# Log decays of a gated linear attention: running sums by VectorE in place of matmuls with level matrices

## The chip, the core and the metric

One Trainium2 chip, one core. A time is the device time of one execution in microseconds (us), lower is better. Engines: PE is TensorE, DVE VectorE, ACT ScalarE, POOL GpSimd, SP SyncE, whose queue issues the DMAs. "PEld" is PE's weight load.

## What is computed

One layer of a hybrid decoder on 256 prompt tokens and 8 x 4 sample tokens (288 columns in all). The change touches the gated linear attention (GLA) only, 4 heads of key dim 256 and value dim 512:

```python
log_a = jax.nn.log_sigmoid((ag @ w_a2 + b_a).astype(f32)) / GLA_GATE_NORM     # GATE_NORM 16
...
b = jnp.cumsum(log_a, axis=2)                 # along the tokens of a chunk
b_last = b[:, :, -1:]
q_i = q * jnp.exp(b)
k_i = k * jnp.exp(-b)
k_d = k * jnp.exp(b_last - b)
A = jnp.where(causal, jnp.einsum('bnlhk,bnmhk->bnhlm', q_i, k_i), 0.0)
o_intra = jnp.einsum('bnlhm,bnmhv->bnlhv', A, v)
...
S = dc[..., None] * S + jnp.einsum('blhk,blhv->bhkv', kc, vc)
```

Both kernels compute it in an equivalent form with another chunking: products of two decays are taken at four levels (across the two blocks of 128 tokens, across halves of 64, across halves of 32, inside 32), so that every exponent is a difference of sums over a short stretch.

## The kernel before

**The frame.** `gemm` multiplies every weight of the layer with the 288 columns. A weight chunk `raw` (128x1024) is loaded by SP, each half is split into `whi` (ACT, a cast, L226) and `wlo` (DVE, raw minus whi, L172), and PE runs 12 matmuls of 288 columns on it (L248 to L250: high with high, high with low, low with high, for four output tiles). `whi` and `wlo` have 5 buffers each; a `gemm` owns 4 PSUM tiles "mm", one for each output tile, and the next `gemm` uses the same four. DVE empties each (`ya<-mm`, `sgg<-mm`) at the end of a `gemm`, so the next `gemm`'s first matmul into a tile waits for that. Its first and last chunks go tile by tile, so that the four tiles end one after another.

**GLA between the chunks.** `gla(h)` and `gla_sample(h)` are generators: `pump` runs them a step at a time between chunks, 1.25 and 0.5 steps for each chunk. So each engine's queue, which it works off strictly in order, holds weight splits and GLA work mixed. Where in the mix an instruction stands is set by the framework's scheduler at build time. The heads 0 to 3 start in the gemms gs2, ps0, gg0 and gg2.

**The decays before.** `gla` computes the gate with tokens on partitions: `pl` (two matmuls of 256 columns, L601) and `pls` (sample tokens, L602), then `log_sigmoid` (three activations and one DVE operation for each), then a split into `lah` and `lal`. Sums along the tokens are matmuls with constant 0, 1/16, -1/16 matrices: for each of the two key halves t and each block, `lah` and `lal` meet `lev` (512 columns, L634) in the bank `pc`, whose columns come out with keys on partitions. ACT takes exp of all 512 columns into `e`, exp of the negative of 128 into `en`, and for block 1 `kd` and `tot`. DVE multiplies these by q and k, and PE forms the score bank `pa` (L662 to L673). `gla_sample` does the same for the sample tokens with `levs` and the bank `pcs` (L730), whose four records for a head are two matmuls.

**Small loads.** POOL issues `norms`, `ident`, `bm` and `levs` near the start, SP `lraw` (the source of `lev`) behind the first gemm's weights. The next head's gate weights `w2r` (buffer of their own) are loaded by SP.

Of the kernel before, what the change touches and what calls it, by code (L numbers as in the profile page):

```python
# [19 lines left out]
P = 128  # L20
# [66 lines left out]
def constants():  # L87
# [28 lines left out]
    c["masks"] = ms.reshape(P, 4 * 288)  # L116
    s, o = t[:, None], t[None, :]
    a = 1.0 / 16.0
    l128a = np.where(s > o, a, 0)
    l128b = np.where(s <= o, a, 0)  # L120

    def level(w):
        blk = (s // (2 * w)) == (o // (2 * w))
        up = (o % (2 * w)) >= w
        sup = (s % (2 * w)) >= w
        return np.where(blk & up & sup & (s <= o), a, 0) + np.where(blk & ~up & ~sup & (s > o), a, 0)

    mid = 15
    same = (s // 32) == (o // 32)
    dg = np.where(same & (o % 32 > mid) & (s % 32 > mid) & (s <= o), a, 0) - np.where(  # L130
        same & (o % 32 < mid) & (s % 32 <= mid) & (s > o), a, 0)
    lv = [level(64), level(32), dg]
    c["lev"] = np.concatenate([l128a] + lv + [l128b], axis=1).astype(f)
    ts = np.arange(TS)
    s, o = ts[:, None], ts[None, :]
    sb = (s // NS) == (o // NS)
    c["levs"] = np.concatenate([np.where(sb & (s <= o), a, 0), np.where(sb & (s > o), a, 0)], axis=1).astype(f)
    rep = t % 32
    c["bm"] = np.concatenate([
# [8 lines left out]
def step_kernel(ctx: ExitStack, tc: tile.TileContext, a: dict):  # L148
# [10 lines left out]
    def bank(name):  # L159
        return psm.tile([P, 512], F32, name=name, tag="sm")  # L160
# [10 lines left out]
    def sub(out, x, y, eng=V):  # L171
        eng.tensor_tensor(out, x, y, ALU.subtract)  # L172
# [404 lines left out]

    def log_sigmoid(ps, n, w, tag, bufs=1):
        t = gpool.tile([P, w], F32, name="ls", tag=tag, bufs=bufs)
        S.activation(t[:n], ps, AF.Abs)  # L580
        S.activation(t[:n], t[:n], AF.Exp, scale=-1.0)
        S.activation(t[:n], t[:n], AF.Ln, bias=1.0)
        V.scalar_tensor_tensor(t[:n], ps, 0.0, t[:n], ALU.min, ALU.subtract)
        return t

    def gla(h):
        zq, zk = (lambda t: zqk[h][:, t]), (lambda t: zqk[h][:, 2 + t])
        yield
        w2r = gpool.tile([P, 256], F32, name="w2r")
        w2 = gpool.tile([P, 256], F32R, name="w2")  # L590
# [7 lines left out]
        yield  # L598
        pl, pls = bank("pl"), bank("pls")
# [26 lines left out]
        for t in range(2):  # L626
            e = main.tile([P, 8, P], F32, name="e", tag=f"Za{2 + t}")
            en = gpool.tile([P, 2, P], F32, name="en", tag="en", bufs=2)
            kd = gpool.tile([P, 2, P], F32, name="kd", tag="kd", bufs=2)
            tot = gpool.tile([P, 2], F32, name="tot", tag="tot", bufs=2)  # L630
            for blk in range(2):
                pc = bank("pc")
# [21 lines left out]
            mul(ev[:, :, 2], ev[:, :, 2], q2)
            mul(en, en, k2)
            mul(kd[:, 1], kd[:, 1], k2[:, 1])
            V.tensor_scalar(kd[:, 0], e[:, 0], tot[:, 1:2], None, ALU.mult)
# [57 lines left out]
    def gla_sample(h):  # L715
        zk = lambda t: zqk[h][:, 2 + t]
        while h not in ready:
            yield
        vr, las = ready[h]
        vs = gpool.tile([P, 512], F32R, name="vs")  # L720
# [12 lines left out]
        pc3 = pc[:, :128].rearrange("p (a b) -> p a b", a=2)  # L733
# [327 lines left out]
```

## Time and profile before

| what | value |
|---|---|
| median of 3 runs | 1817.43 us (1816.79 to 1817.61) |
| the profiled execution: its time, its span | 1817.1 us, 1815.3 us |
| PE busy | 1799.6 us, 99% |
| DVE busy | 1090.0 us, 60% |
| ACT busy | 862.1 us, 47% |
| POOL busy | 84.9 us, 5% |
| granted TensorE clock | nine tenths or more in every slice |

Busy time is the union of an engine's instructions. The chain of waits is followed back from the last instruction, in each step to what released it; its pieces add up to the span. Where an engine's instructions overlap (each is drawn with its fill and drain), the distance from one start to the next, called a step below, is what one costs its queue.

### The profile page before, as it was taken

The numbers are of one execution on the slowest core, as the hardware profiler recorded it, in microseconds if no ns is written. First come the engines' busy times: TensorE is split into PE (matmuls) and PEld (weight loads), VectorE is DVE, ScalarE is ACT, GpSimd is POOL, SyncE is SP. The second block draws the span as 40 slices with busy tenths as digits, with TensorE's granted clock in tenths as the row PEclk, the third lists the DMA queues.
The fourth block names the chain that finished last, engine by engine and source line by source line (L and its number), as shares of the span: only waits on it lengthen the run. The fifth ranks groups of instructions, "written<-read, shape, count | busy, mean of one in ns | idle before, by whom it ended". The sixth has DMA issues, their size and how long they took to land.

```text
span 1815.3 us, 34272 instructions
## 1 busy us (share of the span) xinstructions
PE 1799.6 (99%) x13551; PEld 1754.0 (97%) x13551; DVE 1090.0 (60%) x2004; ACT 862.1 (47%) x1618; POOL 84.9 (5%) x97
## 2 busy tenths in 40 slices
PE   8999999999999999999999999999999999999997
PEld 7999998998999989999999999999999999999997
DVE  7886575675665666766567554455545554455544
ACT  5566464443453654654444553345433553345443
POOL 2000000100100101000023000000000000000002
PEclk9999999999999999999999999999999999999999
DMA  7735447657557466544654555444454555444452
GB/s 271 244 117 165 138 156 244 205 172 246 186 186 261 146 217 242 164 166 154 225 169 162 169 161 167 169 166 163 163 171 166 163 163 173 165 163 165 161 174 87
DMA packets 92304, 324.31 MB, mean 179 GB/s; under 512 B 11056, under 2 KB 12752, under 8 KB 92144
## 3 DMA queue, kind: packets, MB, share of 16 engines
q1 hardware_dynamic: 91728, 321.26, 52.6%
q8 instruction: 106, 1.74, 0.4%
q10 hardware_dynamic: 288, 0.74, 0.1%
q14 instruction: 54, 0.44, 0.1%
q0 software_dynamic: 128, 0.14, 0.0%
HBM read 298.43 MB, written 23.66 MB: 177 GB/s over the span
## 4 chain that ended last, share of the span: by engine, by line
PE 98%; DVE 1%; DMA 0%; ACT 0%; DVEq 0%; SPq 0%; issue 0%
PE mm L248 30%; PE mm L250 30%; PE mm L249 30%; PE pu L781 1%; PE pos L772 1%; PE pst L702 1%; PE score L397 0%; PE pc L634 0%; PE po L695 0%; PE ssq L258 0%; DMA x<-in_x 0%; PE pt L426 0%; DVE wlo L172 0%; PE o L436 0%; DVE x L166 0%; PE pa L668 0%
## 5 line engine op out<-in xcount | busy, mean ns | idle before, releaser
L172 DVE TENSOR_TENSOR wlo<-raw,whi 128x512 fp32r<-128x512 f32 x1040 | 722.5, 706 | 621.0 <-ACT whi L226 618.9
L226 ACT CAST whi<-raw 128x512 fp32r<-128x512 f32 x1040 | 632.2, 619 | 852.7 <-PE mm L249 804.5
L248 PE MATMUL mm<-hh,whi 128*128 128x288 f32 x1472 | 440.1, 299 | 1.2 <-ACT whi L226 1.2
L250 PE MATMUL mm<-hh,wlo 128*128 128x288 f32 x1472 | 433.8, 295 | 2.3 <-DVE wlo L172 2.2
L249 PE MATMUL mm<-hl,whi 128*128 128x288 f32 x1472 | 433.5, 295 | 0.0
L250 PE MATMUL mm<-uh,wlo 128*128 128x288 f32 x1024 | 302.0, 295 | 0.0
L250 PE MATMUL mm<-h2h,wlo 128*128 128x288 f32 x1024 | 301.9, 295 | 0.0
L248 PE MATMUL mm<-h2h,whi 128*128 128x288 f32 x1024 | 301.9, 295 | 0.0
L248 PE MATMUL mm<-uh,whi 128*128 128x288 f32 x1024 | 301.9, 295 | 0.0
L249 PE MATMUL mm<-ul,whi 128*128 128x288 f32 x1024 | 301.7, 295 | 0.0
L249 PE MATMUL mm<-h2l,whi 128*128 128x288 f32 x1024 | 301.7, 295 | 0.0
L248 PEld LDWEIGHTS mm<-hh,whi 128*128 128x128 f32 x1472 | 276.3, 188 | 6.8 <-issue 2.2
L250 PEld LDWEIGHTS mm<-hh,wlo 128*128 128x128 f32 x1472 | 276.1, 188 | 3.5 <-DVE wlo L172 3.0
L249 PEld LDWEIGHTS mm<-hl,whi 128*128 128x128 f32 x1472 | 276.3, 188 | 2.7 <-issue 0.7
L250 PEld LDWEIGHTS mm<-uh,wlo 128*128 128x128 f32 x1024 | 192.3, 188 | 0.0
L250 PEld LDWEIGHTS mm<-h2h,wlo 128*128 128x128 f32 x1024 | 192.3, 188 | 0.0
L249 PEld LDWEIGHTS mm<-ul,whi 128*128 128x128 f32 x1024 | 192.1, 188 | 0.1
L249 PEld LDWEIGHTS mm<-h2l,whi 128*128 128x128 f32 x1024 | 192.1, 188 | 0.1
L248 PEld LDWEIGHTS mm<-h2h,whi 128*128 128x128 f32 x1024 | 192.0, 188 | 0.1
L248 PEld LDWEIGHTS mm<-uh,whi 128*128 128x128 f32 x1024 | 192.0, 188 | 0.1
L250 PE MATMUL mm<-yh,wlo 128*128 128x288 f32 x256 | 75.5, 295 | 0.0
L250 PE MATMUL mm<-gh,wlo 128*128 128x288 f32 x256 | 75.5, 295 | 0.0
(276 smaller groups left out, 1834.2 us busy)
## 6 DMA issues: line engine op xcount, KB each, us to landing
raw<-in_w SPq DMA_DIRECT2D x519, 512.0 KB, 3.3
raw<-in_s SPq DMA_DIRECT2D x32, 512.0 KB, 4.3
out_ssn<-raw SPq DMA_DIRECT2D x32, 512.0 KB, 2.8
x<-in_x SPq DMA_DIRECT2D x4, 576.0 KB, 5.9
out_sp<-so SPq DMA_DIRECT2D x8, 256.0 KB, 2.4
x<-in_x SPq DMA_DIRECT2D x7, 288.0 KB, 7.7
kc<-in_kc SPq DMA_DIRECT2D x2, 512.0 KB, 5.1
out_kcn<-kc SPq DMA_DIRECT2D x2, 512.0 KB, 5.8
```

The lines of the kernel that those rows point to most:

```text
L172: eng.tensor_tensor(out, x, y, ALU.subtract)
L226: S.copy(hi, raw)
L248: T.matmul(o, lhsT=hi[:, sl], rhs=xh(k), start=k == 0, stop=False)
L249: T.matmul(o, lhsT=hi[:, sl], rhs=xl(k), start=False, stop=False)
L250: T.matmul(o, lhsT=lo[:, sl], rhs=xh(k), start=False, stop=k == nk - 1)
L702: T.matmul(pst, lhsT=kdt[:, blk, P * t:P * t + P], rhs=vt[:, blk], start=blk == 0, stop=blk == 1)
L772: T.matmul(pos[r:r + 32], lhsT=qm[:, t, 32 * (b0 + g):32 * (b0 + g) + 32], rhs=st[g][:, 512 * t:512 * t + 512], start=b0 == 0, stop=b0 == ...
L781: T.matmul(pu, lhsT=km[:, P * t:P * t + P], rhs=vs, start=True, stop=True)
```

## The change

The gate is computed with keys on partitions at once (`w2` becomes the stationary operand, `zag` with all 288 tokens the moving one, one bank for each key half). `running` is DVE's running sum: it goes along the columns, multiplies the sum so far by `keep` (0 at the start of each run of 32 prompt tokens or 4 sample tokens, else 1) and adds the next column. The level sums are then differences of these prefix sums `pfx` and of the ends of runs, made by DVE; the factor 1/16 moves into the exponentials. `lev`, `levs`, their loads, `lah`, `lal`, `pls`, `pc` and `pcs` are gone; `seg` (128x288, 144 KB) takes the place of `levs` (32x64, 8 KB) in POOL's queue. `w2r` shares the buffer of `vtok`, so a next head's load waits until the last state matmul of the head ahead has read `vtok`; behind it in SP's queue stands that state's own store. `gla` has one more yield.

```diff
+    c["seg"] = np.tile(np.where(tok < TP, tok % 32 != 0, tok % NS != 0).astype(f), (P, 1))
...
-    G.dma_start(levs, a["levs"])
+    G.dma_start(seg, a["seg"])
...
-        SY.dma_start(lraw, a["lev"])
-        S.copy(lev, lraw)
...
+    def running(out, keep, x):
+        V.tensor_tensor_scan(out, keep, x, 0.0, ALU.mult, ALU.add)
...
-        w2r = gpool.tile([P, 256], F32, name="w2r")
+        w2r = gpool.tile([P, 256], F32, name="w2r", tag="vtok")
...
-        for blk in range(2):
-            T.matmul(pl[:, 256 * blk:256 * blk + 256], lhsT=zag[:, P * blk:P * blk + P], rhs=w2, start=True, stop=True)
-        T.matmul(pls[:TS, :256], lhsT=zag[:, TP:NT], rhs=w2, start=True, stop=True)
-        la = log_sigmoid(pl, P, 512, "A")
-        las = log_sigmoid(pls[:TS, :256], TS, 256, "las", 2)
-        S.copy(lah, la)
-        sub(lal, la, f(lah))
+        for t in range(2):
+            pl = bank("pl")
+            T.matmul(pl[:, :NT], lhsT=w2[:, P * t:P * t + P], rhs=zag, start=True, stop=True)
+            las.append(log_sigmoid(pl[:, :NT], NT, "AB"[t]))
+            running(pfx[:, t], seg, las[t])
...
-                for i, x in enumerate((lah, lal)):
-                    T.matmul(pc, lhsT=x[:, 256 * blk + P * t:256 * blk + P * t + P], rhs=lev[:, P * blk:P * blk + 512],
-                             start=i == 0, stop=i == 1)
-                S.activation(flat(e[:, 4 * blk:4 * blk + 4]), pc, AF.Exp)
-                S.activation(en[:, blk], pc[:, d0:d0 + P], AF.Exp, scale=-1.0)
-                    V.tensor_copy(tot[:, 0:1], pc[:, 511:512])
-                    S.activation(kd[:, 1], pc[:, 384:512], AF.Exp, scale=-1.0, bias=tot[:, 0:1])
+            add(cs[:, :, 0:5:4], end[:, :, 0:4:2], end[:, :, 1:4:2])
+            V.tensor_copy(cs[:, :, 1:6:4], end[:, :, 1:4:2])
+            add(cs[:, :, 2:4], cs[:, :, 0:2], cs[:, :, 4:5].broadcast_to([P, 2, 2]))
+            S.activation(tot, cs[:, 1, 2:3], AF.Exp, scale=GATE)
+            sub(far, cs[:, :, 2:6].unsqueeze(3).broadcast_to([P, 2, 4, 32]), px)
+            sub(l64[:, :, 0:2], cs[:, :, 0:2].unsqueeze(3).broadcast_to([P, 2, 2, 32]), px[:, :, 0:2])
+            V.tensor_copy(l64[:, :, 2], px[:, :, 2])
+            add(l64[:, :, 3], px[:, :, 3], end[:, :, 2:3].broadcast_to([P, 2, 32]))
+            sub(dg, px, px[:, :, :, 15:16].broadcast_to([P, 2, 4, 32]))
+            sub(l32[:, :, 0:4:2], end[:, :, 0:4:2].unsqueeze(3).broadcast_to([P, 2, 2, 32]), px[:, :, 0:4:2])
+            V.tensor_copy(l32[:, :, 1:4:2], px[:, :, 1:4:2])
+            running(e[:, 6], ones, las[t][:, P:TP])
+            S.activation(flat(en), flat(e[:, 4:6]), AF.Exp, scale=-GATE)
+            S.activation(flat(e), flat(e), AF.Exp, scale=GATE)
...
-            T.matmul(pc[:, 64 * t:64 * t + 64], lhsT=las[:TS, P * t:P * t + P], rhs=levs, start=True, stop=True)
-        S.activation(es, pc3, AF.Exp)
-        S.activation(ens, pc3[:, :, 0:TS], AF.Exp, scale=-1.0)
+        sub(ens.rearrange("p a (b c) -> p a b c", c=NS), ps4[:, :, :, NS - 1:NS].broadcast_to([P, 2, NB, NS]), ps4)
+        S.activation(es[:, :, 0:TS], ps, AF.Exp, scale=GATE)
+        S.activation(es[:, :, TS:64], ens, AF.Exp, scale=GATE)
+        S.activation(ens, ps, AF.Exp, scale=-GATE)
```

On PE, where head 0's sample keys `kdr` are turned (`pks`): the program before has a level product (`pc`, block 1 of the first key half) right ahead of it.

```order
L249 MATMUL mm<-hl,whi 128x288
L250 MATMUL mm<-hh,wlo 128x288
L634 MATMUL pc<-lev,lah 128x512
L634 MATMUL pc<-lev,lal 128x512
L749 MATMUL pks<-ident,kdr 128x128 x2
L248 MATMUL mm<-hh,whi 128x288
```

And the program now, at the same turning (`pa` here is the sample tokens' score bank):

```order
L231 MATMUL mm<-hl,whi 128x288
L232 MATMUL mm<-hh,wlo 128x288
L739 MATMUL pks<-ident,kdr 128x128 x2
L745 MATMUL pa_3276<-qi,kir 128x32 x2
L230 MATMUL mm<-hh,whi 128x288
```

The level product is gone, and the two sample score matmuls, which came 24 gemm matmuls later, stand behind `pks`.

On DVE, where gemm gs2 ends in head 0 and its four tiles `mm` are emptied into `ya`, the program before reads:

```order
L166 TENSOR_TENSOR kdr<-zqk_2169,es 128x128
L172 TENSOR_TENSOR wlo<-raw,whi 128x512 x2
L166 TENSOR_TENSOR e<-e,zqk_2169 128x128
L166 TENSOR_TENSOR ya<-mm,rstd_75 128x288 x4
L172 TENSOR_TENSOR wlo<-raw,whi 128x512 x2
L640 COPY tot<-pc 128x1
```

And the program now, at the same emptying, which begins some 40 rows behind the rows `pfx<-seg,ls`:

```order
L155 TENSOR_TENSOR wlo<-raw,whi 128x512
L149 TENSOR_TENSOR e<-e,zqk_2165 128x2x64
L605 MEMSET pa 128x384
L149 TENSOR_TENSOR e<-e,zqk_2165 128x4x32 x2
L149 TENSOR_TENSOR e<-e,zqk_2165 128x256
L149 TENSOR_TENSOR ya<-mm,rstd_74 128x288
L149 TENSOR_TENSOR kd<-e,zqk_2165 128x128
L647 TENSOR_SCALAR kd<-e,tot 128x128
L149 TENSOR_TENSOR ya<-mm,rstd_74 128x288
```

The first emptying now has the whole preparation and six of the multiplications of the first key half ahead of it, and the four emptyings have other work between them.

## Rows read from the trace of the kernel before

**Rows 1.** The page's first lines: the span, and each engine's busy time, share and instructions.

```profile
span 1815.3 us, 34272 instructions
PE 1799.6 (99%) x13551; PEld 1754.0 (97%) x13551; DVE 1090.0 (60%) x2004; ACT 862.1 (47%) x1618; POOL 84.9 (5%) x97
```

**Rows 2.** The chain that ended last, its share by engine.

```profile
PE 98%; DVE 1%; DMA 0%; ACT 0%; DVEq 0%; SPq 0%; issue 0%
```

**Rows 3.** Who waited for whom over the whole span: us in total, times, longest.

```profile
ACT whi L226 <- PE mm L249: 804.5, 774, 3.1
...
PE mm L250 <- DVE wlo L172: 2.2, 2, 1.7
...
PE mm L248 <- ACT whi L226: 1.2, 1, 1.2
```

**Rows 4.** The chain in order of time in head 0 (start, us, what), and its last `pc` piece, in head 3; between the rows are the gemm's matmuls.

```profile
234.88 0.23 PE pl L601 x2
235.11 0.12 PE pls L602
...
246.08 0.58 PE pcs L730 x4
246.67 0.33 PE mm L248
...
250.05 0.46 PE pc L634 x2
...
253.69 0.47 PE pc L634 x2
...
254.38 0.14 PE mm L248
...
257.80 0.48 PE pa L755 x4
...
647.97 0.46 PE pc L634 x2
```

**Rows 5.** The matmuls of the tile `pc`: count, ns min/median/max, first and last start.

```profile
L634 PE MATMUL pc<-lev,lal x16: 393/394/397, 250.1 to 648.0; 128*128 128x512 f32 x16
```

**Rows 6.** Busy time of each engine in a stretch of head 0 and one of head 3 (us, instructions in brackets).

```profile
239.00:261.00 22.00, 22.00 (x184) 21.25 (x184) 18.37 (x45) 17.15 (x34) 0.00 (x0) 1.00 0.39 127
...
614.00:638.00 24.00, 24.00 (x181) 23.48 (x180) 19.86 (x46) 19.89 (x37) 0.00 (x0) 1.00 0.40 132
```

**Rows 7.** Groups of DVE instructions by shape over the whole span: count, then busy us, mean ns of one, idle before.

```profile
L172 DVE TENSOR_TENSOR wlo<-raw,whi 128x512 fp32r<-128x512 f32 x1040 | 722.5, 706 | 621.0 <-ACT whi L226 618.9
...
L942 DVE SCALAR_TENSOR_TENSOR ur<-mm,rstd 128x288 f32<-128x288 f32 x64 | 29.2, 456 | 6.9 <-PE mm L250 6.5
...
L907 DVE SCALAR_TENSOR_TENSOR h2l<-x,norms,h2h 128x288 fp32r<-128x288 f32 x16 | 10.9, 681 | 0.5
...
L172 DVE TENSOR_TENSOR lal<-ls,lah 128x512 fp32r<-128x512 f32 x4 | 2.8, 692 | 0.1
L583 DVE SCALAR_TENSOR_TENSOR ls<-pl,ls 128x512 f32<-128x512 f32 x4 | 2.8, 690 | 3.5 <-ACT ls L582 3.4
...
L583 DVE SCALAR_TENSOR_TENSOR ls<-pls,ls 32x256 f32<-32x256 f32 x4 | 1.6, 400 | 0.0
```

**Rows 8.** DVE in order of time in head 0 (start, us, idle before it in square brackets).

```profile
239.08 0.69 DVE L583 SCALAR_TENSOR_TENSOR ls<-pl,ls 128x512 f32<-128x512 f32 x1 [2.95 <-ACT ls L582]
...
248.33 0.23 DVE L166 TENSOR_TENSOR qi<-zqk,es 128x64 f32<-128x64 f32 x1 [0.37 <-ACT es L734]
248.47 0.28 DVE L166 TENSOR_TENSOR kir<-zqk,ens 128x128 f32<-128x128 f32 x1
...
252.93 0.46 DVE L166 TENSOR_TENSOR ya<-mm,rstd 128x288 f32<-128x288 f32 x1 [0.34 <-PE mm L250]
...
255.31 0.15 DVE L640 COPY tot<-pc 128x1 f32<-128x1 f32 x1
255.38 1.43 DVE L166 TENSOR_TENSOR e<-e,zqk 128x128 f32<-128x128 f32 x6
256.72 0.42 DVE L166 TENSOR_TENSOR en<-en,zqk 128x256 f32<-128x256 f32 x1
```

**Rows 9.** DVE in order of time in head 1.

```profile
363.01 0.45 DVE L166 TENSOR_TENSOR ya<-mm,ya 128x288 f32<-128x288 f32 x1
363.38 0.68 DVE L172 TENSOR_TENSOR wlo<-raw,whi 128x512 fp32r<-128x512 f32 x1
...
366.85 1.39 DVE L172 TENSOR_TENSOR vs<-pvs,vs 32x512 fp32r<-32x512 f32 x2
368.26 2.50 DVE L172 TENSOR_TENSOR wlo<-raw,whi 128x512 fp32r<-128x512 f32 x4
```

**Rows 10.** Groups of ACT instructions by shape (columns as in rows 7).

```profile
L943 ACT ACTIVATE us<-ur 128x288 f32<-128x288 f32 x64 | 28.3, 442 | 18.0 <-DVE ur L942 18.0
...
L847 ACT ACTIVATE sgg<-sgg 128x1152 f32<-128x1152 f32 x4 | 4.7, 1167 | 0.0
...
L582 ACT ACTIVATE ls<-ls 128x512 f32<-128x512 f32 x4 | 2.5, 624 | 0.0
...
L582 ACT ACTIVATE ls<-ls 32x256 f32<-32x256 f32 x4 | 1.6, 400 | 0.0
```

**Rows 11.** Busy time in a stretch near the start (the last two columns are the DMA share and GB/s).

```profile
10.00:15.00 5.00, 4.21 (x29) 3.63 (x27) 4.97 (x5) 5.00 (x12) 4.84 (x5) 1.00 1.03 413
```

More of the change, by code (lines that the diff above doesn't have):

```diff
@@ L116, in constants @@
     c["masks"] = ms.reshape(P, 4 * 288)
[L117 to L138, printed above, removed]
+    tok = np.arange(NT)
+    c["seg"] = np.tile(np.where(tok < TP, tok % 32 != 0, tok % NS != 0).astype(f), (P, 1))
+    ts, rep = np.arange(TS), t % 32
     c["bm"] = np.concatenate([
@@ L179, in step_kernel @@
     bm = main.tile([P, 32 + NB + 34], F32, name="bm")
-    levs = main.tile([TS, 64], F32, name="levs")
-    lev = main.tile([P, 640], F32R, name="lev")
+    seg = main.tile([P, NT], F32, name="seg")
     zag = main.tile([P, NT], F32R, name="zag")
@@ L576, in step_kernel, with log_sigmoid @@
     wsel, wsgn = bm[:, 64 + NB:65 + NB], bm[:, 65 + NB:66 + NB]
[L578 to L583, printed above, removed]
-        return t
+    def log_sigmoid(ps, w, tag):
+        t = gpool.tile([P, w], F32, name="ls", tag=tag)
+        S.activation(t, ps, AF.Abs)
+        S.activation(t, t, AF.Exp, scale=-1.0)
+        S.activation(t, t, AF.Ln, bias=1.0)
+        V.scalar_tensor_tensor(t, ps, 0.0, t, ALU.min, ALU.subtract)
+        return t
+    def running(out, keep, x):
+        V.tensor_tensor_scan(out, keep, x, 0.0, ALU.mult, ALU.add)
     def gla(h):
@@ L598, in gla @@
         yield
-        pl, pls = bank("pl"), bank("pls")
-        for blk in range(2):
-            T.matmul(pl[:, 256 * blk:256 * blk + 256], lhsT=zag[:, P * blk:P * blk + P], rhs=w2, start=True, stop=True)
-        T.matmul(pls[:TS, :256], lhsT=zag[:, TP:NT], rhs=w2, start=True, stop=True)
-        la = log_sigmoid(pl, P, 512, "A")
-        las = log_sigmoid(pls[:TS, :256], TS, 256, "las", 2)
-        ready[h] = (vr, las)
-        lah = gpool.tile([P, 512], F32R, name="lah", tag="B")
-        lal = gpool.tile([P, 512], F32R, name="lal", tag="C")
-        S.copy(lah, la)
-        sub(lal, la, f(lah))
+        pfx = gpool.tile([P, 2, NT], F32, name="pfx", tag="pfx", bufs=2)
+        las = []
+        for t in range(2):
[3 more added lines that the diff above has]
+            running(pfx[:, t], seg, las[t])
+        ready[h] = (vr, pfx)
+        yield
         yield
@@ L626, in gla @@
         for t in range(2):
-            e = main.tile([P, 8, P], F32, name="e", tag=f"Za{2 + t}")
+            e = main.tile([P, 9, P], F32, name="e", tag=f"Za{2 + t}")
             en = gpool.tile([P, 2, P], F32, name="en", tag="en", bufs=2)
             kd = gpool.tile([P, 2, P], F32, name="kd", tag="kd", bufs=2)
-            tot = gpool.tile([P, 2], F32, name="tot", tag="tot", bufs=2)
-            for blk in range(2):
-                pc = bank("pc")
-                for i, x in enumerate((lah, lal)):
-                    T.matmul(pc, lhsT=x[:, 256 * blk + P * t:256 * blk + P * t + P], rhs=lev[:, P * blk:P * blk + 512],
-                             start=i == 0, stop=i == 1)
-                S.activation(flat(e[:, 4 * blk:4 * blk + 4]), pc, AF.Exp)
-                d0 = 384 - P * blk
-                S.activation(en[:, blk], pc[:, d0:d0 + P], AF.Exp, scale=-1.0)
-                if blk == 1:
-                    V.tensor_copy(tot[:, 0:1], pc[:, 511:512])
-                    S.activation(kd[:, 1], pc[:, 384:512], AF.Exp, scale=-1.0, bias=tot[:, 0:1])
-                    S.activation(tot[:, 1:2], tot[:, 0:1], AF.Exp)
-                yield
+            tot = gpool.tile([P, 1], F32, name="tot", tag="tot", bufs=2)
@@ new lines, in gla @@
+            cs = gpool.tile([P, 2, 6], F32, name="cs", tag="cs", bufs=2)
+            px = pfx[:, t, 0:TP].rearrange("p (a b c) -> p a b c", a=2, c=32)
+            end = px[:, :, :, 31]
+            add(cs[:, :, 0:5:4], end[:, :, 0:4:2], end[:, :, 1:4:2])
+            V.tensor_copy(cs[:, :, 1:6:4], end[:, :, 1:4:2])
+            add(cs[:, :, 2:4], cs[:, :, 0:2], cs[:, :, 4:5].broadcast_to([P, 2, 2]))
+            S.activation(tot, cs[:, 1, 2:3], AF.Exp, scale=GATE)
+            runs = lambda i: e[:, i:i + 2].rearrange("p a (b c) -> p a b c", c=32)
@@ L653, in gla @@
                 mul(e5, e5, x.rearrange("p a (b c) -> p a b c", b=2)[:, :, :, i:i + 32])
[L654 removed]
+            mul(e[:, 4:6], e[:, 4:6], q2)
             mul(en, en, k2)
[L656 to L657 removed]
+            mul(kd[:, 1], e[:, 1], k2[:, 1])
+            V.tensor_scalar(kd[:, 0], e[:, 0], tot, None, ALU.mult)
             kds.append(kd)
@@ L661, in cross @@
             def cross():
-                T.matmul(pa[:, P:2 * P], lhsT=e[:, 0], rhs=e[:, 7], start=t == 0, stop=t == 1)
+                T.matmul(pa[:, P:2 * P], lhsT=e[:, 0], rhs=e[:, 6], start=t == 0, stop=t == 1)
             if t == 0:
@@ L979, in step_kernel @@
     for t in range(2):
-        final[0](t, pmm.tile([P, 512], F32, name="mm", tag="mm"), "AC"[t])
+        final[0](t, pmm.tile([P, 512], F32, name="mm", tag="mm"), "AF"[t])
 def pack(w):
```

23 lines of the change are left out of this document (12 added, 11 removed).

## The prediction

> **What bounds the kernel now.** I read the busy shares first: PE is busy for 1799.6 of 1815.3 us [rows 1]. A busy share alone proves little, so the chain of waits comes next: 98% of it is PE [rows 2]. Third, who waits for whom: PE's waits for weight halves come to 3.4 us in all, while ACT's casts wait 804.5 us for PE to free a `whi` buffer [rows 3]. So PE sets the time, and DVE and ACT run ahead of it until the five buffers are full, at most 5 x 12 matmuls of 0.14 us, some 8 us. Two things follow. A microsecond taken from PE's queue is worth a microsecond. Work added to DVE or ACT is free as long as their lead lasts, and costs in full once it is used up. The lead is shortest in GLA, where DVE is busy 18.37 of 22 us in head 0 and 19.86 of 24 us in head 3, with PE still full [rows 6]. The granted clock is 1.00 there, and nothing of the change bears on it.
>
> **What leaves PE.** The chain gives the cost of PE's work in its queue, which is the measure that counts, as matmuls overlap.
> - The level products: 16 pieces of two matmuls (16 records of each kind [rows 5]), 0.46 to 0.47 us each [rows 4]: 7.4 us.
> - The sample level products: one piece of 0.58 us for each head, and the gemm matmul behind it takes 0.33 instead of 0.14 us [rows 4]. Behind the turning that stands there now I expect the usual 0.14. Four times 0.77 is 3.1 us.
> - The gate: 0.23 + 0.12 us before [rows 4], two matmuls of 288 columns now, for which I take the gemm's 0.14 us [rows 4]: 0.07 us a head, 0.3 us in all.
>
> Together 10.8 us off PE, 2.7 us a head. This is the whole possible gain: no other engine is on the path, and the casts, exponentials and loads that go were hidden.
>
> **What DVE gets.** From each head go two `ls`, one `lal` (0.690 + 0.400 + 0.692 us [rows 7]) and two small `tot` copies of 0.15 us [rows 8], 2.1 us. To price the new ones I use steps. A 128x512 split takes 2.50/4 = 0.62 us, a 288-column one 0.37 (363.01 to 363.38) [rows 9]; 256 columns take about 0.34 (a 0.42 us row less the 0.08 us overlap of the others), 128 columns 1.34/6 = 0.22, 64 columns 0.14, one column 0.07 [rows 8].
>
> The running sum is in no row. Below it is bounded by the ordinary two-input form at 288 columns, 0.456 us; the nearest slow row of the same form and width has 0.681 us [rows 7]. A sum that carries its result from column to column can hardly be quicker than the ordinary form, so I take the 0.681, a step of 0.60 (0.08 less, as above). As upper bound I take four times the cost of a column: that is (706 - 456)/224 = 1.12 ns [rows 7], 0.32 us for 288, so 0.456 + 3 x 0.32 = 1.42 us, a step of 1.34.
>
> [...]
>
> For each head that is 0.74 us of `ls`, 1.20 of the two long running sums, 0.14 for `ens`, and for each key half 2.16 us of differences: three small ones (0.21), two of 64 columns (0.28), three of 128 (0.66), two of 256 (0.68), a running sum of 128 (0.33, by the same factor as the long one). In all 6.4 us of steps against 1.7 removed: DVE gets 4.7 us more while PE's stretch shortens by 2.7. The 7.4 us of swing meet 3.6 to 4.1 us of idle time in these stretches [rows 6] and what is left of the lead. So it is close, and one place decides.
>
> **Where PE would notice.** Not first at a weight half but at a PSUM tile: the next gemm's first matmul into a tile waits for DVE's emptying, and the new order puts that emptying deep in GLA work. Head 0, worked out: DVE's `ls` starts at 239.08 after waiting for ACT [rows 8]; the six activations are now of 288 columns (442 ns against 624 and 400 [rows 10]), which saves 3 x 0.14, so 238.66. Up to the end of the first emptying stand `ls` 0.74, running sums 1.20, seven weight halves 4.34, `ens` and `qi` 0.28, `vs` 1.39 [rows 9], four sample products of 128 columns (`kir`, `kdr`) 0.88, the first half's differences 2.16, the first part of the second's 1.05, multiplications 2.00 (six of 128, two of 256 columns), a memset 0.37 (as 288 columns) and the emptying 0.37: 14.8 us, ending at 253.4. PE reached the next gemm at 254.38 [rows 4]; without 0.07, 0.77 and 0.93 of removed pieces, and with 0.48 of the sample score that moves ahead, that is 253.1. The four emptyings come 0.3 to 0.5 us late, since a weight half and a difference stand between them. Eight of the new operations wait for a result that DVE has only just made, where the 0.08 us of overlap is lost: 0.6 more. So PE stalls about 1.1 us in head 0, where it now finds DVE waiting (0.34 us of idle time before an emptying [rows 8]). In the other heads `ls` does not start so late, or fewer operations stand ahead of the emptying; the bounds are 0 and 1.1, I take 0.5 each. In all 2.6 us given back.
>
> **The rest.** On ACT the exponentials of a key half, 512 columns and more for each block, become one piece of 1152 columns (1.167 us at that width [rows 10]) and one of 256, and the casts `lah` and `lev` go: less work in longer pieces. It was hidden and stays so unless DVE waits for such a piece (C, below). `seg` brings 136 KB more to a stretch in which the DMA engines are full, at 413 GB/s, while PE still waits for its first data [rows 11]: 0 to 0.33 us, I take 0.2. It is issued behind `norms`, for which ACT waits. The load of `lraw` and its cast go at a time when PE has its lead: nothing. `w2r` now waits in SP's queue for a state matmul, but the store right behind it waits for a copy of that same matmul's result, so it holds back nothing new; the weight loads behind them have six buffers. The four DVE operations and the cast that prepare the next `w2` leave the hot stretch with it, which helps a little and is not counted. The extra yield moves steps by less than a chunk: nothing, covered by the gemm's own matmuls.
>
> **Sum.** The profiled execution took 1817.1 us, its span 1815.3 and 1.8 around it; the median is 0.3 above. 1817.1 - 10.8 + 2.6 + 0.2 = 1809.1, against the median 1809.4 us.
>
> **Rivals.**
> - A, all of it is hidden. For it: in head 0 DVE is only 0.3 to 0.5 us late by plain steps, and a running sum at 0.456 us would take that away; DVE also had idle time there (0.37 and 0.34 us in two rows [rows 8]). Against: the loss of overlap. Time: 1817.4 - 10.8 + 0.2 = 1806.8.
> - B, slower: the running sum is the new bound. Two of 288 and one of 128 columns stand ahead of each first emptying, as much as 2.44 long ones, so every microsecond above the 0.60 step costs four heads 9.8 us. The 8.0 us of net gain are gone at a step of 1.42 us, just above the bound, and the kernel is measurably slower from 1.8. At eight times the cost of a column (0.456 + 7 x 0.32 = 2.7, step 2.6) it would be 1817.4 - 8.0 + 19.6 = 1829. Against it: every DVE form in the rows stays within 1.5 times of the plain one.
> - C, ACT gives the gain back: the exponential of all nine tiles is one piece of 1.167 us where there were pieces of 512 columns, it stands behind casts that wait for PE, and DVE's multiplications, weight halves behind them, wait for it in order. If in each head one of the two is waited for in full, 4.7 us are lost (1814.1), if both, 9.3 us (1818.7). For it: in head 0 DVE already waits 2.95 us for ACT once [rows 8]. Against: the order puts a weight half and the other half's differences, some 2 us of DVE work, between the last difference and the first multiplication.
>
> **How the numbers follow.** The forecast, 1809.4, has 0.52, and its own bounds (0 to 1.1 us in each head, the running sum between 0.456 us and some 0.9, 3 us for four heads) reach from 1807 to 1813; at the upper bound of 1.42 us it would be 1809.4 + 9.8 x 0.74 = 1816.7. A has 0.27, C 0.14, B 0.07. About 0.2%, 3.6 us, is what a measurement can tell from no change. Faster by more (below 1813.8): A, nearly all of the forecast and a quarter of C, 0.81; within it: most of C and edges, 0.12; slower: most of B, 0.07. The range from 1806.0 to 1816.0 takes in A, the forecast, a dear running sum up to nearly its bound and half of C, and leaves out some 0.16.
>
> **What would show it.** No pieces `pc` and `pcs` in the chain and some 10.8 us less PE work: the first step. PE waits in the heads' stretches, ended by DVE's emptying `ya` or `sgg` and by `wlo`, of 2 to 4 us in all: the second; none at all is A, and waits ended by ACT behind DVE's multiplications are C. A row of the running sum at 288 columns near 0.68 us: the price; above 1.4 us is B. DVE busy in head 0's stretch of 22 us near 22. The forecast is wrong above all if DVE's lead at `ls` is another than the trace shows, as then everything behind it shifts by as much.

## The result, and the profile after

The changed kernel takes 1806.75 us (median of 4 runs, 1806.35 to 1807.01) against 1817.37 us of the kernel before, a ratio of 0.9943 (95% interval 0.9931 to 0.9955): 10.6 us are gone. The profiled execution's span went from 1815.3 to 1805.1 us, at a mean granted clock of 0.998.

Line numbers have moved: multiplications are L149 (were L166), subtractions and `wlo` L155 (L172), `whi` L208 (L226), the gemm's matmuls L230 to L232 (L248 to L250).

The page's first lines, and the chain by engine, answer [rows 1, 2]:

```profile
span 1805.1 us, 34198 instructions
...
PE 1789.4 (99%) x13499; PEld 1746.8 (97%) x13499; DVE 1103.2 (61%) x2092; ACT 855.8 (47%) x1593; POOL 84.6 (5%) x97
...
PE 96%; DVE 2%; ACT 1%; issue 0%; DMA 0%; DVEq 0%; SPq 0%; ACTq 0%
```

PE is busy 10.2 us less, DVE 13.2 us more, ACT 6.3 us less. PE still sets the time, but 3% of the chain are now DVE's and ACT's. (The chain runs back through DVE's and ACT's work behind each wait of PE, so these shares are not PE's idle time.) Who PE waits for over the whole span (us in total, times, longest), against [rows 3]:

```profile
PE mm L232 <- DVE wlo L155: 1.8, 2, 1.0
...
PE mm L230 <- DVE ya L149: 1.0, 2, 0.6
PE mm L230 <- ACT whi L208: 0.6, 1, 0.6
```

The wait for `ya`, DVE's emptying of a PSUM tile, is new. The same stretches as [rows 6], with one each of heads 1 and 2 (window and length in us, then busy time and instructions of PE, PE's weight load, DVE, ACT, POOL; granted clock, DMA share, GB/s):

```profile
239.00:261.00 22.00, 21.41 (x163) 21.06 (x162) 21.47 (x66) 16.03 (x31) 0.00 (x0) 1.00 0.34 121
354.00:378.00 24.00, 23.62 (x180) 23.28 (x179) 22.17 (x61) 14.41 (x32) 0.00 (x0) 1.00 0.44 154
488.00:510.00 22.00, 22.00 (x192) 21.00 (x191) 19.93 (x66) 16.17 (x30) 0.00 (x0) 1.00 0.41 144
614.00:638.00 24.00, 23.86 (x202) 22.40 (x201) 23.23 (x72) 17.27 (x32) 0.00 (x0) 1.00 0.47 155
```

PE was full in all four before. Now 0.59 us are missing in head 0, 0.38 in head 1, none in head 2 and 0.14 in head 3, 1.1 us together. DVE fills 21.47 of 22 us in head 0, where it was 18.37.

How PE's time in GLA changed I work out from the distance of each matmul's start to the next one's, added up by tile, from gs2's first matmul to rg1's first. This sum falls from 478.23 to 467.78 us, by 10.45. The removed pieces held 7.74 (`pc`), 2.34 (`pcs`) and 0.47 us (`pls`), and `pl` costs 0.12 more: 10.43. The rest nearly cancels: 1.1 us of new idle time and 1.47 more for `pst` stand against 2.5 less for `pu`, `pk` and `pv`, which have other neighbours now (0.7 of it is `pv`, whose last turning had a sample piece behind it). Ahead of this stretch 0.34 us more, behind it 0.06 less.

### The profile page after: what moved, and what is told of

Read it like the earlier page. It is cut to its first block, busy times and chain, and to the rows that moved or that the text cites. A ratio compares the mean times of both kernels' runs of the same rounds, so it can differ in the third digit from the quotient of the medians.

```text
span 1805.1 us, 34198 instructions
## 1 busy us (share of the span) xinstructions
PE 1789.4 (99%) x13499; PEld 1746.8 (97%) x13499; DVE 1103.2 (61%) x2092; ACT 855.8 (47%) x1593; POOL 84.6 (5%) x97
## 4 chain that ended last, share of the span: by engine, by line
PE 96%; DVE 2%; ACT 1%; issue 0%; DMA 0%; DVEq 0%; SPq 0%; ACTq 0%
PE mm L230 30%; PE mm L232 30%; PE mm L231 30%; PE pu L771 1%; PE pos L762 1%; DVE wlo L155 1%; PE pst L692 1%; PE score L379 0%; PE po L685 0%; DMA raw<-in_w 0%; PE pt L408 0%; PE ssq L240 0%; PE o L418 0%; DVE x L149 0%; ACT whi L208 0%
## 5 line engine op out<-in xcount | busy, mean ns | idle before, releaser
L155 DVE TENSOR_TENSOR wlo<-raw,whi 128x512 fp32r<-128x512 f32 x1040 | 721.4, 705 | 601.1 <-ACT whi L208 599.2
L208 ACT CAST whi<-raw 128x512 fp32r<-128x512 f32 x1040 | 631.7, 619 | 832.5 <-PE mm L231 782.0
L230 PE MATMUL mm<-hh,whi 128*128 128x288 f32 x1472 | 441.2, 300 | 1.2 <-ACT whi L208 0.6
L232 PE MATMUL mm<-hh,wlo 128*128 128x288 f32 x1472 | 434.1, 295 | 2.0 <-DVE wlo L155 1.8
L232 PE MATMUL mm<-h2h,wlo 128*128 128x288 f32 x1024 | 301.9, 295 | 0.0
L232 PE MATMUL mm<-uh,wlo 128*128 128x288 f32 x1024 | 301.9, 295 | 0.0
L230 PE MATMUL mm<-h2h,whi 128*128 128x288 f32 x1024 | 301.8, 295 | 0.0
L230 PE MATMUL mm<-uh,whi 128*128 128x288 f32 x1024 | 301.8, 295 | 0.0
L230 PEld LDWEIGHTS mm<-hh,whi 128*128 128x128 f32 x1472 | 277.1, 188 | 6.0 <-issue 1.7
L232 PEld LDWEIGHTS mm<-hh,wlo 128*128 128x128 f32 x1472 | 276.8, 188 | 3.0 <-DVE wlo L155 2.7
L232 PEld LDWEIGHTS mm<-h2h,wlo 128*128 128x128 f32 x1024 | 192.3, 188 | 0.0
L232 PEld LDWEIGHTS mm<-uh,wlo 128*128 128x128 f32 x1024 | 192.3, 188 | 0.0
L230 PEld LDWEIGHTS mm<-uh,whi 128*128 128x128 f32 x1024 | 192.0, 188 | 0.1
L230 PEld LDWEIGHTS mm<-h2h,whi 128*128 128x128 f32 x1024 | 192.0, 188 | 0.1
L232 PE MATMUL mm<-yh,wlo 128*128 128x288 f32 x256 | 75.5, 295 | 0.0
L232 PE MATMUL mm<-gh,wlo 128*128 128x288 f32 x256 | 75.4, 295 | 0.0
```

The lines of the kernel that those rows point to most:

```text
L208: S.copy(hi, raw)
L230: T.matmul(o, lhsT=hi[:, sl], rhs=xh(k), start=k == 0, stop=False)
L232: T.matmul(o, lhsT=lo[:, sl], rhs=xh(k), start=False, stop=k == nk - 1)
```

## The experiments

**Theory Q**: PE's queue is the whole gain. The removed matmuls gave it, and a little comes back where DVE, out of lead, empties a PSUM tile late (theory D). **Rivals**: the gain came from ACT's and the loads' lighter work (H), or DVE's new work is hidden (A).

The last columns give PE's idle time in GLA, us by head, read from PE in order of time (gaps of 0.05 us or more; the kernel before: none).

| run | median us | ratio to before, 95% interval | head 0 | 1 | 2 | 3 |
|---|---|---|---|---|---|---|
| changed kernel | 1806.75 | 0.9931 to 0.9955 | 0.58 | 0.38 | 0 | 0.14 |
| e11_after | 1806.85 | 0.9933 to 0.9958 | 0.58 | 0.38 | 0 | 0.20 |
| e1_level_back | 1814.30 | 0.9976 to 0.9993 | 0 | 0.38 | 0 | 0.14 |
| e2_sample_back | 1810.12 | 0.9948 to 0.9973 | 0.21 | 0.38 | 0.34 | 0.14 |
| e12_both_back | 1817.44 | 0.9993 to 1.0011 | 0 | 0.38 | 0.29 | 0.14 |
| e3_scan_twice | 1809.96 | 0.9947 to 0.9972 | 0.83 | 1.01 | 0.48 | 1.44 |
| e7_scan_four | 1821.61 | 1.0015 to 1.0033 | 3.02 | 2.73 | 1.47 | 3.63 |
| e4_w2r_own | 1807.53 | 0.9932 to 0.9959 | 1.52 | 0.38 | 0 | 0.14 |
| e5_seg_late | 1806.52 | 0.9931 to 0.9956 | 1.69 | 0.38 | 0 | 0.50 |
| e6_copies_act | 1807.21 | 0.9933 to 0.9961 | 0.58 | 0.38 | 0 | 0.14 |
| e8_first_pool | 1811.52 | 0.9955 to 0.9980 | 2.11 | 0.38 | 0.81 | 1.09 |
| e9_second_behind | 1807.21 | 0.9936 to 0.9960 | 0.11 | 0.38 | 0 | 0.13 |
| e10_both | 1806.98 | 0.9932 to 0.9959 | 0.12 | 0.38 | 0 | 0.14 |

### PE's pieces put back

```diff
+    def level_pair(blk):                      # e1, e12: at two yields of each key half
+        pc = bank("pc")
+        for i in range(2):
+            T.matmul(pc, lhsT=hh[:, 2 * blk + i, 0:P], rhs=flat(hh)[:, 0:512], start=i == 0, stop=i == 1)
...
+        pc = bank("pcs")                      # e2, e12: in gla_sample
+        for t in range(2):
+            T.matmul(pc[:, 64 * t:64 * t + 64], lhsT=ident[:TS, :], rhs=bm[:TS, 0:64], start=True, stop=True)
```

> The changed kernel, and in it 16 pieces of PE work like the level products that the change removed: at two yields of each key half two matmuls of 128x512 in the same number type, into a PSUM bank that nobody reads. No other engine gets anything, and the outputs are computed as before. Theory Q (the gain is PE's queue alone): 16 x 0.46 = 7.4 us come back, less up to 1 us because DVE gets that much more time in stretches where PE now waits for it: 1812.5 to 1814.5 us, and the waits ended by the emptying ya shrink or go. Rival N (the removed pieces cost more than their own time, by the dearer matmul behind each change of kind): 16 x 0.2 = 3 us on top, 1816 to 1818. Rival H (the gain came from the casts, exponentials and loads that left ACT and DVE, and PE's level products were filler): under 1 us, at most 1808.

> The changed kernel with the sample level products back on PE: two matmuls of 32 partitions by 64 columns for each head, of constants, into a bank that nobody reads; outputs as before. Theory Q with the price of my sum (0.58 us for the piece and 0.19 for the dearer matmul behind it): 4 x 0.77 = 3.1 us, 1809.9. Rival: the piece alone counts, 4 x 0.58 = 2.3 us, 1809.1. Rival H: nothing, 1806.8. The time alone hardly tells the first two apart; the rows of the piece and of the matmul behind it in the chain do (0.33 against 0.14 us).

> The changed kernel with both kinds of removed PE work put back as pieces into banks that nobody reads: the 16 level pairs and the 4 sample pairs. All that ACT and DVE lost or got by the change stays as the change made it; outputs as before. Theory Q (PE's queue is the whole of it): 7.5 + 3.4 by the two single runs, less up to 0.5 because DVE's lateness at the emptyings is covered again: 1816.7 to 1817.7, the kernel before to within 0.05%. Rival H (part of the gain came from shorter ACT work or from loads): 1815 or less. Rival X (the new DVE work costs something of its own, which the shorter queue hid): above 1818.

Measured: 7.5 us more with the level pairs, 3.4 with the sample pairs, 10.7 with both, which is the kernel before to 0.02% (interval -0.07% to 0.11%). By starts the 16 level pairs hold 7.40 us, and head 0's idle time is covered again. The sample piece, on PE in head 0 of e2_sample_back (start, us), and below it the same place in the changed kernel:

```profile
245.42 0.60 PE L599 MATMUL pv<-ident,zv 128*128 128x128 f32 x4
245.95 0.65 PE L720 MATMUL pcs<-bm,ident 32*128 32x64 f32 x4
246.53 0.40 PE L230 MATMUL mm<-hh,whi 128*128 128x288 f32 x1
246.77 0.30 PE L231 MATMUL mm<-hl,whi 128*128 128x288 f32 x1
```

```profile
245.29 0.60 PE L599 MATMUL pv<-ident,zv 128*128 128x128 f32 x4
245.65 0.38 PE L230 MATMUL mm<-hh,whi 128*128 128x288 f32 x1
245.86 0.29 PE L231 MATMUL mm<-hl,whi 128*128 128x288 f32 x1
```

From 245.95 to 246.53 are the 0.58 us of [rows 4]. The rest of the price does not stand where I had put it, at the matmul behind: its step is 0.24 us with the piece and 0.21 without. It stands ahead of the piece: the four turnings `pv` take 0.53 us from start to start of what follows, and 0.36 without. Together that is 0.78 us for a head. Q holds, H falls: all that ACT lost and DVE got is still in e12_both_back, and nothing of the gain is, as far as the interval tells (some 2 us). N (16 x 0.2 us on top) falls too. A piece's own 0.58 us alone, 2.3 us in all, is too little for the 3.4 of e2_sample_back.

### Running sums done more often

```diff
     def running(out, keep, x):
-        V.tensor_tensor_scan(out, keep, x, 0.0, ALU.mult, ALU.add)
+        for _ in range(2):                    # e7: 4
+            V.tensor_tensor_scan(out, keep, x, 0.0, ALU.mult, ALU.add)
```

> The changed kernel with every running sum done twice over the same data, which adds 0.66 us of DVE work for 288 columns and about 0.33 for 128, and nothing to any other engine; outputs as before. Some 2.4 long sums stand ahead of the first emptying of each head, 1.6 us. Theory D (DVE's lead is used up in heads 0, 1 and 3, and what is put ahead of the emptyings passes on to PE in full): 4 x 1.6 = 6.5 us where all four heads pass it on, 4.5 where head 2 still hides most: 1811.3 to 1813.3, with PE's waits for ya, sgg and wlo at 5 to 8 us in all instead of about 3. Rival A (DVE's work is hidden, and the small waits in the profile have nothing to do with it): at most 1 us, up to 1807.8.

> The changed kernel with every running sum done four times over the same data, 3 x 0.66 us more for 288 columns and 3 x 0.33 for 128; same values. Some 4.8 us more DVE work ahead of each first emptying. PE's idle time in GLA was 1.1 us with the sum once and 3.8 with it twice, where the price of rival B (9.8 us for each us of step) had asked for 7.6. Theory O (the order is made anew for each kernel and puts emptyings ahead of DVE's multiplications when DVE is late, so a fixed share, some 0.4, passes on): 0.42 x 19.2 = 8 us above the changed kernel, 1814 to 1816. Theory K (each head has a fixed cover, 1.35, 0.97, 1.12 and 0.30 us by the run with the sum twice, and beyond it all passes on): 4 x 4.8 - 3.7 = 15.5 us, 1821 to 1824. The price of rival B as I put it: 9.8 x 1.98 = 19.4, 1826.

Twice costs 3.2 us, less than D had put (4.5 to 6.5), three times what A allows; idle time rises by 2.7 us where 6.4 us of work stand ahead of the emptyings. Of PE's waits there, 1.1 us end with copies of ACT (`vtok` in head 0, `og` in head 2), which D does not speak of:

```profile
PE mm L232 <- DVE wlo L155: 1.4, 1, 1.4
PE pa L746 <- ACT vtok L601: 0.6, 1, 0.6
PE pu L772 <- ACT og L688: 0.5, 1, 0.5
```

Four times costs 14.9 us, near K's 15.5, but not in K's way: idle time rises by 9.7 us only, 0.51 of the 19.2 put ahead, between O's share of 0.4 and K. The other 5 us are PE's clock: in three stretches of some 3 us the steps of its matmuls are longer, by 4.9 us in all. Who PE waits for in GLA with four sums, then head 0 in short stretches (columns as above; the granted clock is the third from the end):

```profile
PE mm L232 <- DVE wlo L155: 8.1, 3, 3.6
PE mm L230 <- DVE ya L149: 2.7, 1, 2.7
```

```profile
243.00:246.80 3.80, 0.83 (x7) 0.60 (x5) 3.74 (x7) 0.76 (x2) 0.00 (x0) 1.00 0.00 0
246.80:248.00 1.20, 1.14 (x6) 1.15 (x7) 1.20 (x7) 1.03 (x4) 0.00 (x0) 0.67 0.27 27
248.00:250.00 2.00, 2.00 (x11) 1.98 (x11) 2.00 (x6) 0.65 (x2) 0.00 (x0) 0.50 0.72 254
250.00:252.00 2.00, 2.00 (x14) 2.00 (x14) 2.00 (x12) 0.82 (x3) 0.00 (x0) 0.84 0.74 256
252.00:254.00 2.00, 2.00 (x18) 2.00 (x17) 1.92 (x5) 1.34 (x3) 0.00 (x0) 1.00 0.82 252
```

The wait is now for a weight half, since 5.29 us of running sums stand in a row there. In all four heads only the two long sums, and not those of 128 columns, stand ahead of what PE waits for, so 3.96 us a head were added there and not 4.8, and 9.7 us are 0.62 of these 15.8. The wait ends at 246.86; from 247.2 the granted clock is 0.50, a matmul's step 0.24 instead of 0.13 us, for some 3 us. After waits of 2.73 us (head 1) and 3.63 (head 3) the same shows (0.50 and 0.52 in 374 to 376 and 631 to 633); after 1.47 us in head 2, and 1.44 in head 3 of e3_scan_twice, it stays at 1.00. Why not all of DVE's added work becomes idle time is partly seen: the order is made anew for each kernel, and with two sums the scheduler put the four emptyings of head 0 between the multiplications, where they stood behind most of them; the first one came only 0.5 us later behind `ls` than in the changed kernel.

### The uncounted preparation of w2, and the load of seg

```diff
-        w2r = gpool.tile([P, 256], F32, name="w2r", tag="vtok")
+        w2r = gpool.tile([P, 256], F32, name="w2r")            # e4
...
-    G.dma_start(seg, a["seg"])                                 # e5
...
         SY.dma_start(flat(wa), a["wa"])
+        SY.dma_start(seg, a["seg"])
```

> The changed kernel with one part undone: the raw copy of w2 has its own buffer again, so that the next head's w2 is loaded and prepared early, within the hot stretch, as in the kernel before. Theory W (the give-back was smaller than forecast because these four DVE operations and a cast had left the hot stretch, which my sum did not count): some 1.2 us of DVE work a head come back ahead of the emptyings, up to 1 to 3 us, 1808 to 1810, and waits for ya and sgg grow. Rival (they were never ahead of an emptying that PE waits for): no difference, 1806.8 within 0.4.

> The changed kernel with the load of seg moved from the start to the place where lraw was loaded before; nothing else differs. Theory G (the load is in the way of the first weights): the gemm gs2 starts at about 222.8 us instead of 223.1, and the time is 0.3 us shorter, 1806.45. Rival: the later start is chance, since the runs with the same start order have gs2 at 222.9 to 223.7: no difference, within 0.3 of 1806.75.

With its own buffer 0.8 us more, and head 0 idles 0.89 instead of 0.58 us at the emptying, with 0.63 more at a matmul `pu`, behind ACT's copies of `og`. The direction is W's, the size below its range; the time alone does not settle it. The load of seg: 1806.52 us, inconclusive. The gate `pl` of head 0 starts at 234.39 us here and at 234.76 in e10_both with seg late, with seg early at 235.05 and 234.75 in the two profiles of the changed kernel, and at 234.72 before the change. Two executions of one kernel differ by more than the term. e5_seg_late also idles 1.1 us at a `pu` in head 0 and 0.36 at one in head 3, with PE and ACT in the very order of the changed kernel, and DVE too from 40 us on. So the order alone does not make that wait. The two profiles of the changed kernel show none in head 0, and e11_after 0.06 us in head 3; the profile of e5_seg_late is the slowest of its five executions (1807.64 us, the fastest 1806.23). What makes it longer is not shown.

### Relief for DVE: less work, another engine, another place

```diff
-            V.tensor_copy(l64[:, :, 2], px[:, :, 2])
+            S.copy(l64[:, :, 2], px[:, :, 2])                  # e6, and the copy into l32
...
-            sub(far, cs[:, :, 2:6].unsqueeze(3).broadcast_to([P, 2, 4, 32]), px)
+            sub(far, cs[:, :, 2:6].unsqueeze(3).broadcast_to([P, 2, 4, 32]), px, G)    # e8, and all of l64
...
+            hold = tc.keep_in_program_order if t == 1 else (lambda ins: ins)           # e9, e10
-            sub(far, ...)
+            hold(sub(far, ...))                                # and the ten others of the second key half
```

> The changed kernel with the two copies of each key half's differences (64 columns a block into the third tile pair, 2 x 32 into the last) made by ACT instead of DVE; the same values. DVE loses 0.11 + 0.14 us of steps for each key half, 0.5 us a head, most of it ahead of the first emptying. Theory D: PE's idle time in GLA, 1.1 us now (0.58 in head 0, 0.38 in head 1, 0.14 in head 3), falls to about 0.5, and the time to 1806.1 to 1806.4. Rival C: ACT, which has casts waiting for PE ahead of the copies, now holds the exponentials up and with them DVE's multiplications: PE idles 1.5 us or more, 1807.2 or above.

> The changed kernel with the first group of each key half's differences (far, the three pieces of l64) made by GpSimd instead of DVE; same values. DVE loses about 0.8 us of steps for each key half. Theory D: PE's idle time in GLA (1.1 us) goes to nearly 0, 1805.6 to 1806.0. Rival P (GpSimd is so much slower at it that the exponentials, DVE's multiplications behind them and the weight halves behind those wait): PE idles 2 us or more, 1808 to 1812, with DVE rows that wait for ACT's exponentials and these for GpSimd.

> The changed kernel with the same work on every engine, where the second key half's differences (11 DVE operations) are kept in the order in which the code is written, so that the scheduler can't put them ahead of the first emptyings; in head 0 the seven that stood ahead of it, 1.0 us of steps, now stand behind. Theory P (place, not amount: PE waits because the scheduler fills DVE's time up to the emptying with whatever is ready, which is why less DVE work alone gave nothing): the first emptying of head 0 comes about 1 us earlier, PE's idle time there goes from 0.58 to 0, in GLA from 1.1 to 0.5 us, 1806.2. Rival T (the emptying waits for something else, as the exponential of nine tiles ahead of the multiplications): 0.58 stays, 1806.75. Rival L (the second half's exponentials and scores come so late that PE waits for them): PE idles 1.5 us or more, 1807.2 or above.

> The run with the second half's differences behind, and seg loaded late as in the run before it. If both gains hold and add: 0.3 to 0.6 us at the start and 0.6 in head 0, 1805.6 to 1805.9, the best kernel here. If the time between the sample products of head 0 and ACT's copies of og (an idle time of 1.1 us in the run with seg late, at a matmul pu) comes with the earlier start, the gain is gone again: 1806.5 to 1807.

> The changed kernel once more, without an edit, to tell how far two runs of one kernel differ. Every theory: 1806.75 within 0.3, PE's idle time in GLA 1.1 us with 0.58 in head 0, 0.38 in head 1 and 0.14 in head 3. If the idle time at pu in some of the other runs (0.3 to 1.1 us) is a matter of chance from execution to execution, it may appear here as well; if it belongs to their order of instructions, it does not. The same for the start of gs2 (222.4 to 223.7 us so far).

With the copies on ACT nothing is gained: the idle times are the same to 0.01 us, and the time is 1807.21 us. D's forecast fails here, and C's idle time is not there either. DVE in order of time in head 0 of e6_copies_act:

```profile
249.71 0.62 DVE L155 TENSOR_TENSOR e<-cs,pfx 128x128 f32<-128x128 f32 x2
250.25 0.42 DVE L155 TENSOR_TENSOR e<-pfx 128x256 f32<-128x256 f32 x1
250.58 0.69 DVE L149 TENSOR_TENSOR e<-e,zqk 128x128 f32<-128x128 f32 x3
...
252.44 0.81 DVE L149 TENSOR_TENSOR e<-e,zqk 128x128 f32<-128x128 f32 x3
253.28 0.46 DVE L149 TENSOR_TENSOR ya<-mm,rstd 128x288 f32<-128x288 f32 x1
```

The first emptying comes 14.43 us after `ls` starts, as in the changed kernel. The time freed is filled: the difference of 256 columns at 250.25, which stood behind the emptyings at 255.47 (below), now stands ahead of them. So in this place the amount is not what counts while the scheduler has something to fill with. e9_second_behind holds just that work back. DVE there:

```profile
249.22 0.41 DVE L149 TENSOR_TENSOR en<-en,zqk 128x256 f32<-128x256 f32 x1
250.07 0.70 DVE L149 TENSOR_TENSOR e<-e,zqk 128x128 f32<-128x128 f32 x3 [0.44 <-ACT e L634]
...
251.94 0.80 DVE L149 TENSOR_TENSOR e<-e,zqk 128x128 f32<-128x128 f32 x3
252.78 0.46 DVE L149 TENSOR_TENSOR ya<-mm,rstd 128x288 f32<-128x288 f32 x1
```

The emptying comes 0.47 us earlier behind `ls` (13.96 us) and head 0 idles 0.11 us: theory P, as far as the place goes. It did not come the whole 1 us earlier, as DVE now waits 0.44 us for the exponential of nine tiles, so T has a part in it. And the time does not fall, against P: 1807.21 us, and 1806.98 in e10_both, which shows no gain either though it has no wait at `pu`; the changed kernel once more took 1806.85. The idle time saved is spent elsewhere: by starts, GLA takes 467.90 us against 467.78 and 467.85 in the changed kernel's two profiles. The gemm matmuls take 0.5 us more, some of it in two more changes between score pieces and gemm. No version here beats the changed kernel by more than its own executions differ (1806.35 to 1807.59 us).

GpSimd is too slow for the differences, rival P. Its groups in head 0 of e8_first_pool (count, then us busy, mean ns, idle before), and waits there:

```profile
L155 POOL TENSOR_TENSOR e<-cs,pfx 128x256 f32<-128x256 f32 x2 | 2.2, 1117 | 0.2
L155 POOL TENSOR_TENSOR e<-cs,pfx 128x128 f32<-128x128 f32 x2 | 1.0, 516 | 4.8 <-DVE cs L618 4.8
```

```profile
PE pa L745 <- ACT vtok L600: 1.3, 1, 1.3
ACT e L633 <- POOL e L155: 1.2, 1, 1.2
...
PE mm L230 <- DVE ya L149: 0.8, 1, 0.8
```

DVE needs 418 ns for the 256 columns, GpSimd 1117; ACT's exponential waits for it 1.2 us, and PE then in two places. Here too the granted clock falls to 0.50 (258 to 260 us), after idle times of 1.29 and 0.82 us within 1.5 us.

## Why the prediction was right, point by point

**PE's queue, 10.8 us: right, a little low.** Both kinds of pieces put back cost 10.7 us. By starts the level products are 7.74 us (priced at 7.4; 7.5 put back), the gate 0.35 (0.3), and the sample products of all four heads 2.34 of their own and 0.78 at their edges, 3.1 as priced (3.4 put back). But that price was right by luck in one part: I read 0.33 us for the matmul behind the piece and expected 0.14 now. By starts it went from 0.24 to 0.21 in head 0, and the rest came off the turnings `pv` ahead. Other neighbours, a term that I did not have, give 0.3 more (1.47 dearer at `pst`, 1.8 cheaper at `pu` and `pk`). Together 11.5 us.

**DVE's late emptying: the mechanism right, the size not.** Head 0 in order, first DVE, then PE:

```profile
238.93 0.82 DVE L562 SCALAR_TENSOR_TENSOR ls<-pl,ls 128x288 f32<-128x288 f32 x2 [2.47 <-ACT ls L561]
239.67 1.40 DVE L566 TENSOR_TENSOR_SCAN pfx<-seg,ls 128x288 f32<-128x288 f32 x2
...
250.67 0.69 DVE L149 TENSOR_TENSOR e<-e,zqk 128x128 f32<-128x128 f32 x3
...
252.53 0.80 DVE L149 TENSOR_TENSOR e<-e,zqk 128x128 f32<-128x128 f32 x3
253.36 0.46 DVE L149 TENSOR_TENSOR ya<-mm,rstd 128x288 f32<-128x288 f32 x1
253.74 0.28 DVE L149 TENSOR_TENSOR kd<-e,zqk 128x128 f32<-128x128 f32 x1
253.94 0.28 DVE L647 TENSOR_SCALAR kd<-e,tot 128x128 f32<-128x128 f32 x1
254.13 0.45 DVE L149 TENSOR_TENSOR ya<-mm,rstd 128x288 f32<-128x288 f32 x1
254.50 0.68 DVE L155 TENSOR_TENSOR wlo<-raw,whi 128x512 fp32r<-128x512 f32 x1
255.10 0.45 DVE L149 TENSOR_TENSOR ya<-mm,rstd 128x288 f32<-128x288 f32 x1
255.47 0.42 DVE L155 TENSOR_TENSOR e<-pfx 128x256 f32<-128x256 f32 x1
255.80 0.45 DVE L149 TENSOR_TENSOR ya<-mm,rstd 128x288 f32<-128x288 f32 x1
```

```profile
252.54 0.38 PE L739 MATMUL pks<-ident,kdr 128*128 128x128 f32 x2
252.76 0.53 PE L745 MATMUL pa<-qi,kir 128*128 128x32 f32 x4
253.88 0.40 PE L230 MATMUL mm<-hh,whi 128*128 128x288 f32 x1 [0.58 <-DVE ya L149]
```

(Eight multiplications of the first key half stand ahead of the first emptying, as my sum had it: six of 128 columns and two of 256.) I had `ls` at 238.66 and the emptying's end at 253.4, plus 0.6: 254.0. It starts at 238.93 and the emptying ends at 253.82. PE, forecast there at 253.1, is free at 253.30 and stalls 0.58 us. The 1.1 us forecast for head 0 included the three later emptyings; they come 0.7 to 1.0 us apart, and PE's first chunk goes tile by tile, so none is waited for. **The term that was mis-sized is the 2.6 us given back**: 1.1 were measured. In heads 1 to 3 I took 0.5 us each between bounds of 0 and 1.1; they are 0.38, 0 and 0.14. In head 1 only `ls` and the two long running sums stand ahead of the emptying that PE waits for, and in head 3 the wait is for a weight half. As a sign I had named 2 to 4 us of waits, and 1.1 are there.

How the 2.65 us between forecast (1809.4) and result (1806.75) come about: for the profiled execution the two are 2.2 us apart (1809.1 forecast, 1806.9 measured). Of these 1.5 are the give-back and 0.7 PE's queue (11.5 instead of 10.8), less 0.1 at the start. The other 0.45 us are the distance of the profiled executions from the medians. The range holds the result by 0.75 us only, at the edge that was put there for A.

**DVE's new work: right.** I had 4.7 us of steps a head, 18.8 in all. The durations of all DVE instructions sum to 24.4 us more (1187.8 against 1163.4); less 0.08 us of overlap for each of 88 additional ones that is 17.4, an estimate. Busy time rose by only 13.2, since more of them now follow each other without a gap and overlap.

**The running sum: 0.681 us was a little low.** Its rows (ns min/median/max):

```profile
L566 DVE TENSOR_TENSOR_SCAN pfx<-seg,ls x8: 728/738/748, 239.7 to 613.3; 128x288 f32<-128x288 f32 x8
L566 DVE TENSOR_TENSOR_SCAN e<-ones,ls x8: 410/420/422, 248.4 to 632.2; 128x128 f32<-128x128 f32 x8
```

738 ns at 288 columns, a step of 0.66 (5.29 us for eight in e7_scan_four), where I took 0.60. The 0.06 us of step that I was short are 0.15 us ahead of a first emptying, less than these runs tell.

**A, all hidden (1806.8)**, gives the measured time but not the profile: the waits ended by `ya` are there, and e3_scan_twice shows that DVE's work is not free. That its number came out is chance: 1.1 us of idle time are balanced by 0.7 us more from PE's queue and by the distance of profile and median.

**B, the running sum as bound**: the mechanism exists (e7_scan_four is slower than before), the price was wrong. I had 9.8 us for each us of step; the first 0.66 us cost 3.2, the next 1.32 cost 11.7, 5 of them through the clock. By those two runs the point from which it is slower than before lies at a step of about 2.1 us (an estimate: 1.32 + 1.32 x 7.1/11.7, as if the cost were even between the two runs), not 1.42.

**C, ACT's long exponential**: DVE waits for it four times, once a head, 4.0 us in all. These waits (at 262.6, 386.5, 509.3 and 635.4 us) stand well behind the places where PE idles (253.9, 364.7 and 616.2 us), and PE has no gap at them. Only e9_second_behind, with other work out of the way, shows 0.44 us of it ahead of an emptying.

**The rest.** `seg` at 0.2 us stays open between 0 and 0.3. The preparation of `w2`, "not counted", is worth at most 0.8 us.

## What to carry to other kernels

Take the gain from the queue of the engine that is full, by the distance of starts, and prove it by putting dummies of the removed work back: here they cost 10.7 us where 10.6 had been gained. Before relieving an engine that is waited for, look at what the scheduler has ready for the freed time: 0.5 us of work taken off DVE moved the emptying by nothing, while holding back work that is not urgent moved it by 0.47 us. Then look at the time itself: here it did not fall with the idle time. Price added work on an engine with a lead by two runs: the first 6.4 us put ahead cost 3.2 here, the next 12.8 cost 11.7.

## What was unexpected

Idle time of PE is not the whole price of a wait: after each of the three waits of 2.73 to 3.63 us in e7_scan_four PE ran some 3 us at a granted clock of 0.50, with a matmul's step of 0.24 instead of 0.13 us, and 5 of the 14.9 us come from that. The idle times of 0.58, 0.38 and 0.14 us came out alike to 0.01 us in both profiles of the changed kernel and in e6_copies_act: they belong to the order of instructions, not to chance.
